# Which engine makes the low halves of the split weights: VectorE alone in four phases

## The chip, the cores and the metric

One core of a Trainium2 chip runs the whole program. The metric is the device time of one execution in microseconds, median of several runs. The engines are named as the profile names them: PE (TensorE, matrix products; PEld is its weight load), DVE (VectorE), ACT (ScalarE), POOL (GpSimd) and SP, whose queue issues the weight DMAs.

## What is computed

Three transformer layers over 256 tokens of width 1024, all float32. Layer 0 mixes with eight forget-gate heads and eight sparse heads, layer 1 with sixteen causal heads, and each is followed by a gated FFN of width 2816 with a short convolution. Layer 2 mixes with eight latent-attention heads and four mLSTM heads, and is followed by a mixture of 32 experts and a gated embedding.

```python
def conv_glu_ffn(x, w_up, conv_w, conv_b, w_down):
    h = x @ w_up
    g, u = h[..., :D_FF], h[..., D_FF:]
    g = conv(g, conv_w) + conv_b            # causal, three taps, per channel
    return (jax.nn.silu(g) * u) @ w_down

for layer in range(2):
    h = rmsnorm(x, attn_norm[layer])
    x = x + mixer(h @ w_in[layer]) @ w_out[layer]
    x = x + conv_glu_ffn(rmsnorm(x, ffn_norm[layer]), w_up[layer], ..., w_down[layer])
x = rmsnorm(x, final_norm)
h = rmsnorm(x, norm_mix_g)
x = x + concat(latent_attention, mlstm)(h @ w_in_2) @ w_o
x = x + moe(rmsnorm(x, norm_ffn_g))
x = x + (p @ w_ple) * sigmoid(rmsnorm(x, norm_ple_g) @ w_ple_gate)
return rmsnorm(x, final_norm_g)
```

## The kernel before

**Split products.** A dense product is made of three: with a = ah + al and w = wh + wl, where the high parts are roundings to the PE's fast float32 type and the low parts are the remainders, it is ah·wh + al·wh + ah·wl. A unit is one 128 x 1024 piece of weight. `Weights.high` (L291) has ACT round a unit into `wh`, and `Weights.low` (L300) subtracts that from the loaded weight `w` into `wl`. Both inputs of that subtraction lie in SBUF. The subtraction is cut in eighths of a unit's first free dimension: `W.eighths` of eight go to POOL and the others to DVE, two instructions one behind the other in program order, each on its own engine. Some buffers of both kinds are a spare tile called `extra`, and the output projections use `xhw`, `xlw` and `wo` for some units.

**Who sets the share.** `W.eighths` begins at 0, is 3 from L1486 on for the first mixer, takes `SHARE[0]` = 3 when a mixer is done (L1578, so for the FFN behind it), `SHARE[1]` = 5 at the last of an FFN's 22 column blocks (L1313), `SHARE[2]` = 4 in the second mixer (L1594), `SHARE[3]` = 4 in the third (L1676), and 3 for the last gate (L2457). In the tail of every output projection (L1198) and in a forced piece at the end of the first FFN (L1303) it is 0.

**Phases.** The first mixer with its output projection (to about 150 us), the first FFN (to 331), the second mixer and its output projection (to about 460), the second FFN (to 649), the third mixer's input projection (to 706), its output projection and router (to about 780), and then the experts and the gate. An FFN (`ffn`, L1235) goes over 22 blocks of 128 columns. `up(j)` multiplies two units, `gate` does convolution and gating on ACT and DVE (the DVE steps write `more`, three times `c`, and `al`), and `down(j)` multiplies one unit by `ah` and `al`. That is 72 matmuls of 128x256 for a block. The four phases that the change touches have 66 + 32 + 66 + 12 units.

**Order of the work.** All instructions are placed by a planner at build time: `Clock` (L64) gives each a cost (L142 to L146: DVE 0.07 us + 1.04 ns for each column of a subtraction, POOL 0.1 us + 2.2 ns) and keeps a time for each engine. `prepare` (L320) converts units ahead of their use, and `tick` (L432) places steps of the attention and norm chains between matmuls, but none while the planned time of ACT or DVE is over `LEAD` (8, 4 and 4 us) ahead of the PE's (L445). So other costs can give another order. Each engine runs its instructions strictly in the order placed. `W.done` frees a weight's slot after its last low part, and the next weight DMA on SP's queue waits for that.

In the profile all records carry the line of the recording helper, L205, so rows are told apart by their tiles.

Of the kernel before, what the change touches and what calls it, by code (L numbers as in the profile page):

```python
# [26 lines left out]
NEG = -1e30  # L27
SW = 2064
EARLY = (2.0, 3.0, 1.5)
SHARE = (3, 5, 4, 4)  # L30
SIDE = (2, 6, 3)
FIRST = 3
WARM = 10
# [315 lines left out]
def kc(t, k, c):  # L349
    return t[:, :k * c].rearrange("p (k c) -> p k c", k=k)  # L350
# [3 lines left out]
def tile_two_blocks(ctx: ExitStack, tc: tile.TileContext, a: dict, out: bass.AP):  # L354
# [6 lines left out]
    def st(shape, dt=F32, tag=None, name=None, bufs=1):  # L361
        return sb.tile(list(shape), dt, tag=tag or name, name=name or tag, bufs=bufs)
# [3 lines left out]
    def bank(i):  # L366
        t = ps.tile([128, 512], F32, tag=f"b{i}", name=f"bank{i}", bufs=1)
        if i == 7:
            last_misc[0] = t
        return t  # L370
# [5 lines left out]
    def mm(o, l, r, start, stop):  # L376
        nc.tensor.matmul(o, l, r, start=start, stop=stop, skip_group_check=True)
# [4 lines left out]
    def tt(o, x, y, op=OP.mult, eng=None):  # L382
        (eng or nc.vector).tensor_tensor(o, x, y, op=op)
# [17 lines left out]
    W = Weights(nc, sb, NS)  # L401
# [7 lines left out]
    lay = [0]  # L409
# [22 lines left out]
    def tick(most=None, lead=None):  # L432

        n = 0
        most = most or MOST[lay[0]]
        lead = lead or LEAD[lay[0]]
        for w in [w for w in waiting if w[1] <= state]:
            waiting.remove(w)
            go(w[0])
        for p in [p for p in parting if p[1] <= state]:  # L440
            parting.remove(p)
            W.drop(*p[0])
        W.prepare(clk)
        for e in list(side):
            if n == most or max(clk.at["act"], clk.at["dve"]) > clk.now() + lead:  # L445
                break
            if e[1] <= clk.now() + SLACK[lay[0]] and step(e):
                n += 1
        return n
# [3 lines left out]
    def pause():  # L453

        if tick(1, 1e9):
            idle[0] = 0
            return
        idle[0] += 1
        if idle[0] > 400:
            raise RuntimeError("side work is stuck")  # L460
        clk.floor = clk.now() + 0.1
# [23 lines left out]
    def free(*names):  # L485
        busy.difference_update(names)
        for n in names:
            freed[n] = clk.last
# [9 lines left out]
    def drain():  # L498
        while side or waiting:
            pause()  # L500
# [478 lines left out]
    def norm_of(sums, rope=None):  # L979

        yield sums.left[-1][1]
        rsqrt(rt, sums.done()[:, :, 0], D, 2)
        yield
        spread(rb, rt)
        if rope is not None:
            rope_scaled(rope, rb)


    def product(o, u, m, start, bh=None, bl=None):

        bh, bl = (xh, xl) if bh is None else (bh, bl)
        h, l = W.take(u, clk)
        hv, lv = kc(h, KD, 128), kc(l, KD, 128)
        until(l)
        for k in range(KD):
            mm(o[:m], hv[:, k, :m], bh[:, k], start and k == 0, False)
            mm(o[:m], hv[:, k, :m], bl[:, k], False, False)
            mm(o[:m], lv[:, k, :m], bh[:, k], False, k == KD - 1)
            if k % 2:
                tick()  # L1000
# [3 lines left out]
    def halves_of(b):  # L1004
        return b.rearrange("p (a t) -> p a t", a=2)
# [3 lines left out]
    def dense_bank(keep=False):  # L1009

        dn[0] ^= 1
        n = ("dense", dn[0])
        while n in busy:
            pause()
        b = halves_of(bank(5 + dn[0]))
        if keep:
            busy.add(n)
            owner[b.tensor.name] = n
        return b
# [125 lines left out]
    def out_proj(us, pair_done, mixed):  # L1145

        nonlocal xh, xl
        for i, t in enumerate(("xh", "xl")):  # L1150
            W.places[us[2 + i]] = sb.tile([128, 2, 1024], F32R, tag=t, name=f"{t}w", bufs=1)
        room = HOLD[lay[0]]
        if room:
            W.places[us[4]] = W.hold("wo", (128, 2, 1024), F32R)
        begun = []
        for m in (0, 2):
            b = dense_bank()
            begun.append((b, us[m:m + 2], list(range(KD))))
        own = None
        for u in us[:2]:  # L1160
            W.pairs[u] = W.take(u, clk)
        W.more = 2 + room
        W.once = ONCE
        while any(left for _, _, left in begun):
            if not own and len(side) <= SIDE[lay[0]] and not waiting and W.parted[1] > us[4 + room]:
                own = next((n for n in BK[2:] if n not in busy and freed.get(n, 0.0) <= clk.now()), None)
                if own:
                    busy.add(own)
                    begun.append((halves_of(bank(own[1])), us[4:5 + room], list(range(KD))))
            k = None  # L1170
            for b, un, left in begun:
                if W.parted[1] <= un[-1]:
                    continue
                ws = [W.pairs[u] for u in un]
                k = next((k for k in left if ("mixed", lay[0], k) in state and
                          (not side or max(clk.ready(ml[:, k]), clk.ready(ws[-1][1])) <= clk.now() + SLACK[lay[0]])), None)
                if k is not None:
                    break
            if k is not None:
                for i, (h, l) in enumerate(ws):  # L1180
                    hv, lv = kc(h, KD, 128), kc(l, KD, 128)
                    mm(b[:, i], hv[:, k], mh[:, k], len(left) == KD and i == 0, False)
                    mm(b[:, i], lv[:, k], mh[:, k], False, False)
                for i, (h, l) in enumerate(ws):
                    mm(b[:, i], kc(h, KD, 128)[:, k], ml[:, k], False, len(left) == 1)
                left.remove(k)
                tick()
            else:
                pause()
        for u in us[:4]:  # L1190
            W.take(u, clk)
        W.more, W.once = 0, False
        drain()
        mixed()
        if lay[0] < 2:
            xh = st([128, KD, T], F32R, tag="xh", name="xh")
            xl = st([128, KD, T], F32R, tag="xl", name="xl")
        e, W.eighths = W.eighths, LASTS  # L1198
        for m in range(0, KD, 2):
            if m < 4:  # L1200
                b = begun[m // 2][0]
            else:
                b = begun[2][0] if own and m == 4 else dense_bank()
                for i in range(2):
                    if own and m == 4 and i <= room:
                        W.take(us[m + i], clk)
                    else:
                        product(b[:, i], us[m + i], 128, i == 0, mh, ml)
            tt(X[:, m:m + 2], b, X[:, m:m + 2], OP.add)
            if not m:  # L1210
                for u in us[5 + room:6 + 2 * room]:
                    W.force(0, u)
                    W.force(1, u)
            if m == NXT and room and lay[0] < 2:
                W.force(0, us[7] + 1)
                W.force(1, us[7] + 1)
            pair_done(m)
            if m == 4 and room:
                W.drop("wo")
            if m == 4 and own:  # L1220
                free(own)
        W.eighths = e
# [12 lines left out]
    def ffn(l, us, norm, pair_done, limit_after):  # L1235
# [21 lines left out]
        def up(j):  # L1257
            b = halves_of(bank(4 + j % 3))
            product(b[:, 0], us[j][0], 128, True)
            product(b[:, 1], us[j][1], 128, False)  # L1260
            if j == 0:
                finish(norm)
            g = gate(j, b)
            next(g)
            go(g)
# [43 lines left out]
        def ups(j):  # L1309
            if j == NJ - 9:  # L1310
                W.limit = limit_after
            if j == NJ - 1:
                W.eighths = SHARE[1]  # L1313
            up(j)
# [259 lines left out]
    def mixed(*names):  # L1574
        def go_on():
            dbg("mh" if not lay[0] else f"mh{lay[0]}", mh.bitcast(F32))
            W.limit = NS
            W.eighths = SHARE[0]  # L1578
            W.drop(*names)
        return go_on  # L1580

    sums = Sums()
    out_proj(PL["wo0"], fed_by(lambda k: col("ffn_norm", k), sums), mixed("V", "aP", "aPT", "aQ", "a1", "a2"))
    W.drop("mh", "ml")
    dbg("X1", X)
# [7 lines left out]
    lay[0] = W.phase = 1  # L1593
    W.eighths = SHARE[2]  # L1594
    norm = norm_of(sums, 0)
# [18 lines left out]
    for i in range(8):  # L1614
# [5 lines left out]
        go(moba(i, qks[i % 3], b))  # L1620
    sums = Sums()
    out_proj(PL["wo1"], fed_by(lambda k: col("ffn_norm", 8 + k), sums), mixed("V", "aP", "aPT", "aQ", "aR"))
    W.drop("mh", "ml")
    dbg("X3", X)
# [50 lines left out]
    W.limit = NS - 9  # L1675
    W.eighths = SHARE[3]  # L1676
    cq = halves_of(aP[:, 1536:2048])
# [916 lines left out]
```

## Time and profile before

| | |
|---|---|
| median of 3 runs | 1067.29 us (1064.92 to 1072.06) |
| the profiled execution | 1074.68 us, of it 1073.0 us span |
| PE, DVE, ACT, POOL busy in the span | 998.9, 632.5, 476.1, 357.4 us |
| mean granted clock of TensorE | 0.962 |

The span runs from the first instruction to the last. A busy PE is not a PE at its peak: matmuls are pipelined, a 128x256 one is recorded with about 280 ns and the next begins some 115 ns behind it. So the number of matmuls in a stretch tells more than the busy time. The granted clock is a share of full speed, 0.5 being 1.2 GHz and 1.0 being 2.4 GHz.

### The profile page before, as it was taken

How to read it: one execution, taken by the hardware profiler on the slowest of the kernel's cores; microseconds unless marked ns; L12 is line 12 of the kernel's file. 1: busy time of each engine (PE TensorE's matmuls, PEld its weight loads, DVE VectorE, ACT ScalarE, POOL GpSimd, SP SyncE). 2: the span in 40 equal slices, each digit the busy share in tenths (PEclk: the TensorE clock that was granted, in tenths of full speed). 3: DMA queues.
4: the chain of work that ended last, by engine and by line, in shares of the span. 5: the costliest groups of instructions: out<-in, count | busy, mean ns of one | idle time of the engine just before them, and what ended most of it. 6: DMA issues, size and time to landing. Idle time of an engine off the chain costs nothing. (4 is left out here: it accounts for less than half of the span.)

```text
span 1073.0 us, 19846 instructions
## 1 busy us (share of the span) xinstructions
PE 998.9 (93%) x7612; PEld 857.0 (80%) x7612; DVE 632.5 (59%) x1285; ACT 476.1 (44%) x866; POOL 357.4 (33%) x365
## 2 busy tenths in 40 slices
PE   7999999999998998999999999879989999798686
PEld 7888899999998987999999999867874554353456
DVE  4798577676677589676666687567552221021056
ACT  5555565455554555464554555644512121121053
POOL 7424154445545433344544453341310000000032
PEclk8999999999999999999999999979989999998888
DMA  7653299465511541497556103330879999999951
GB/s 214 167 193 119 79 345 345 155 218 171 183 41 38 160 144 54 162 370 254 182 172 210 53 1 93 105 118 23 311 277 334 351 412 410 410 412 411 401 183 40
DMA packets 135318, 223.14 MB, mean 208 GB/s; under 512 B 11161, under 2 KB 103473, under 8 KB 135217
## 3 DMA queue, kind: packets, MB, share of 16 engines
q1 hardware_dynamic: 134673, 221.80, 58.4%
q8 instruction: 62, 1.02, 0.4%
q14 instruction: 39, 0.32, 0.1%
q10 hardware_dynamic: 544, 0.00, 0.0%
HBM read 220.73 MB, written 1.05 MB: 207 GB/s over the span
## 5 line engine op out<-in xcount | busy, mean ns | idle before, releaser
L205 PE MATMUL bank<-xh,wh 128*128 128x256 f32 x808 | 233.9, 289 | 3.0 <-ACT wh L205 3.0
L205 PE MATMUL bank<-xl,wh 128*128 128x256 f32 x808 | 228.3, 283 | 0.8 <-DVE xl L205 0.8
L205 PE MATMUL bank<-xh,wl 128*128 128x256 f32 (+1 forms) x752 | 212.6, 283 | 5.1 <-DVE wl L205 5.1
L205 POOL TENSOR_TENSOR wl<-w,wh 128x384 fp32r<-128x384 f32 (+2 forms) x97 | 141.1, 1461 | 199.9 <-ACT wh L205 92.7
L205 ACT ACTIVATE wh<-w 128x1024 fp32r<-128x1024 f32 x153 | 159.5, 1050 | 8.6 <-PE bank L205 5.4
L205 PEld LDWEIGHTS bank<-xh,wh 128*128 128x128 f32 x808 | 155.4, 192 | 5.5 <-ACT wh L205 3.3
L205 PEld LDWEIGHTS bank<-xl,wh 128*128 128x128 f32 x808 | 155.1, 192 | 2.5 <-DVE xl L205 1.4
L205 PEld LDWEIGHTS bank<-xh,wl 128*128 128x128 f32 (+1 forms) x752 | 143.7, 191 | 6.0 <-DVE wl L205 6.0
L205 PE MATMUL bank<-xh,extra 128*128 128x256 f32 (+1 forms) x552 | 141.7, 283 | 0.0
L205 PE MATMUL bank<-w,xg 128*32 128x512 f32 (+1 forms) x512 | 93.9, 647 | 17.8 <-DMA w<-in_w_up_e_dram 11.6
L205 PEld LDWEIGHTS bank<-xh,extra 128*128 128x128 f32 (+1 forms) x552 | 98.9, 188 | 0.7 <-issue 0.7
L205 POOL TENSOR_TENSOR gate<-w,gate 128x384 fp32r<-128x384 f32 x8 | 11.5, 1466 | 253.2 <-DMA w<-in_w_down_e_dram 235.7
L205 DVE TENSOR_TENSOR wl<-w,wh 128x640 fp32r<-128x640 f32 (+3 forms) x102 | 87.7, 861 | 9.9 <-ACT wh L205 6.9
L205 PEld LDWEIGHTS bank<-w,xg 128*32 128x32 f32 (+1 forms) x512 | 30.4, 127 | 72.0 <-issue 71.6
L205 ACT ACTIVATE c<-more,v,cw 128x256 f32<-128x256 f32 x44 | 26.5, 603 | 132.9 <-DVE more L205 132.9
L205 POOL TENSOR_TENSOR extra<-w,wh 128x384 fp32r<-128x384 f32 (+2 forms) x49 | 64.5, 1317 | 41.8 <-ACT wh L205 32.4
L205 DVE TENSOR_TENSOR more<-bank,more 128x512 f32<-128x512 f32 x44 | 30.3, 689 | 77.2 <-PE bank L205 77.2
L205 DVE SCALAR_TENSOR_TENSOR sg<-sg,ws,bank 128x256 f32<-128x256 f32 x11 | 5.3, 480 | 115.9 <-ACT sg L205 115.9
L205 PE MATMUL bank<-al,wh 128*128 128x256 f32 x256 | 71.7, 280 | 1.2 <-DVE al L205 1.2
L205 PE MATMUL bank<-ah,wh 128*128 128x256 f32 x256 | 71.4, 279 | 0.0
L205 PE MATMUL bank<-xl,extra 128*128 128x256 f32 (+2 forms) x248 | 69.8, 281 | 0.0
L205 PE MATMUL bank<-ah,extra 128*128 128x256 f32 x256 | 65.7, 280 | 1.5 <-DVE extra L205 1.5
(484 smaller groups left out, 2385.4 us busy)
## 6 DMA issues: line engine op xcount, KB each, us to landing
w<-in_w_up_dram SPq DMA_DIRECT2D x44, 1024.0 KB
w<-in_w_gate_e_dram SPq DMA_DIRECT2D x64, 512.0 KB
w<-in_w_up_e_dram SPq DMA_DIRECT2D x64, 512.0 KB
w<-in_w_down_e_dram SPq DMA_DIRECT2D x32, 1024.0 KB
w<-in_w_down_dram SPq DMA_DIRECT2D x22, 1024.0 KB
w<-in_w_in_odd_dram SPq DMA_DIRECT2D x12, 1024.0 KB
w<-in_w_in_even_dram SPq DMA_DIRECT2D x9, 1024.0 KB
w<-in_w_in_dram SPq DMA_DIRECT2D x5, 1024.0 KB
```

What stands on the lines that cost most here:

```text
L205: return f(*a, **kw)
```

## The change

In both FFNs, the second mixer and the third mixer's input projection DVE makes the whole low part of each unit in one 128x1024 subtraction, and POOL none of it. In the first mixer, the third mixer's output projection and the last gate the shares stay as they were.

```diff
-SHARE = (3, 5, 4, 4)
+SHARE = (0, 0, 0, 0)
...
         own = None
+        if lay[0] == 2:
+            W.eighths = 4
         for u in us[:2]:
             W.pairs[u] = W.take(u, clk)
```

The second piece stands in `out_proj`: `lay[0]` is the layer, so it gives the third mixer's output projection the 4 that it had from `SHARE[3]` before.

## Rows read from the trace of the kernel before

**Rows 1.** The page's first part: busy us of each engine (share) xinstructions.

```profile
PE 998.9 (93%) x7612; PEld 857.0 (80%) x7612; DVE 632.5 (59%) x1285; ACT 476.1 (44%) x866; POOL 357.4 (33%) x365
```

**Rows 2.** Windows by stage: us, busy us (xcount) of five engines, clock, DMA share, GB/s.

```profile
160.00:320.00 160.00, 160.00 (x1377) 160.00 (x1376) 112.23 (x156) 81.88 (x116) 78.21 (x57) 1.00 0.56 189
320.00:345.00 25.00, 20.71 (x157) 19.89 (x156) 21.07 (x33) 14.12 (x25) 12.75 (x9) 0.93 0.00 1
345.00:460.00 115.00, 110.88 (x931) 103.51 (x930) 83.16 (x169) 60.73 (x137) 47.75 (x32) 0.99 0.43 143
460.00:640.00 180.00, 179.56 (x1526) 179.56 (x1527) 127.25 (x185) 92.82 (x131) 86.17 (x64) 0.99 0.54 177
640.00:706.00 66.00, 59.71 (x447) 55.35 (x446) 47.44 (x106) 38.73 (x60) 24.75 (x21) 0.97 0.31 97
```

**Rows 3.** PE's waits from 135 to 706 us: us in total, times, longest.

```profile
PE bank L205 <- DVE wl L205: 6.0, 3, 3.2
PE bank L205 <- DVE extra L205: 4.9, 3, 1.7
PE bank L205 <- DVE al L205: 1.2, 2, 0.6
PE bank L205 <- DVE xl L205: 1.1, 3, 0.5
PE bank L205 <- DVE rt L205: 1.0, 2, 0.6
```

**Rows 4.** Timeline of PE: start, us, instruction, idle time before it and releaser.

```profile
326.93 0.39 PE L205 MATMUL bank<-ah,wl 128*128 128x256 f32 x1 [1.71 <-DVE wl L205]
...
644.65 0.39 PE L205 MATMUL bank<-ah,extra 128*128 128x256 f32 x1 [1.46 <-DVE extra L205]
...
679.59 0.38 PE L205 MATMUL bank<-xh,wl 128*128 128x256 f32 x1 [3.22 <-DVE wl L205]
```

**Rows 5.** DVE's groups by shape, 160 to 320 us: busy us, mean ns | idle before.

```profile
L205 DVE TENSOR_TENSOR c<-c,more 128x256 f32<-128x256 f32 x20 | 25.4, 1271 | 0.0
L205 DVE TENSOR_TENSOR wl<-w,wh 128x640 fp32r<-128x640 f32 x28 | 23.0, 821 | 0.1
L205 DVE SCALAR_TENSOR_TENSOR c<-more,cw,c 128x256 f32<-128x256 f32 x39 | 18.9, 485 | 1.2 <-ACT c L205 0.5
L205 DVE TENSOR_TENSOR al<-c,ah 128x256 fp32r<-128x256 f32 x20 | 14.7, 733 | 9.7 <-ACT ah L205 9.7
L205 DVE TENSOR_TENSOR more<-bank,more 128x512 f32<-128x512 f32 x20 | 13.8, 690 | 36.7 <-PE bank L205 36.7
```

**Rows 6.** A DVE group by shape over the whole span, away from the FFNs.

```profile
L205 DVE TENSOR_TENSOR more<-more,more 128x256 f32<-128x256 f32 x6 | 2.3, 422 | 5.8 <-ACT more L205 5.8
```

**Rows 7.** POOL's largest group by shape, 160 to 320 us.

```profile
L205 POOL TENSOR_TENSOR wl<-w,wh 128x384 fp32r<-128x384 f32 x28 | 40.3, 1441 | 59.5 <-DVE c L205 36.0 <-ACT wh L205 22.6 <-DVE extra L205 0.8
```

**Rows 8.** Timeline of DVE: a low part that DVE makes whole.

```profile
136.86 1.22 DVE L205 TENSOR_TENSOR wl<-w,wh 128x1024 fp32r<-128x1024 f32 x1
```

**Rows 9.** Timeline of DVE at the first FFN's end.

```profile
320.78 0.56 DVE L205 TENSOR_TENSOR extra<-w,wh 128x384 fp32r<-128x384 f32 x1
321.38 1.68 DVE L205 TENSOR_TENSOR c<-c,more 128x256 f32<-128x256 f32 x1
323.60 1.17 DVE L205 TENSOR_TENSOR al<-c,ah 128x256 fp32r<-128x256 f32 x1 [0.55 <-ACT ah L205]
324.69 2.17 DVE L205 TENSOR_TENSOR wl<-w,wh 128x384 fp32r<-128x384 f32 x1
```

**Rows 10.** Timeline of DVE, the second mixer's output projection.

```profile
429.50 1.78 DVE L205 TENSOR_TENSOR xlw<-w,xlw 128x512 fp32r<-128x512 f32 x1
```

**Rows 11.** Timeline of POOL in the same stretch.

```profile
428.99 1.74 POOL L205 TENSOR_TENSOR wo<-w,wo 128x512 fp32r<-128x512 f32 x1
```

**Rows 12.** Timeline of DVE in the third mixer, ahead of the longest wait.

```profile
675.26 2.60 DVE L205 SCALAR_TENSOR_TENSOR bX<-bX,v 128x253 f32<-128x253 f32 x3 [0.33 <-ACT bX L205]
```

**Rows 13.** Windows, columns as above: two stretches with a lowered clock.

```profile
339.00:343.00 4.00, 4.00 (x22) 4.00 (x23) 1.53 (x9) 0.40 (x2) 0.00 (x0) 0.57 0.00 0
...
711.00:729.00 18.00, 16.64 (x57) 12.88 (x58) 5.25 (x11) 6.78 (x18) 5.40 (x5) 0.53 0.23 76
```

## The prediction

> **What bounds the kernel now.** I read the page's first part, then windows by stage, then PE's waits, then the timelines around the waits. On the page PE is busy for 93% of the span, DVE for 59%, POOL for a third [rows 1]. The windows tell where that is no slack and where it is [rows 2]. In the 160 us of the first FFN's steady part PE has no idle time: 1377 matmuls, so 0.116 us each, and the second FFN's stretch is the same but for 0.4 us at its start. A block of 72 matmuls takes 72 x 0.116 = 8.4 us, and no faster low part can shorten that. The change must earn its time elsewhere: 4.3 us of PE idle time at the first FFN's end, 4.1 in the second mixer, 6.3 in the third's input projection [rows 2]. The waits name what ends these: from 135 to 706 us PE waits 6.0 + 4.9 us for low parts (`wl` and `extra`, three waits each) and 1.2 us for `al`, and 2.1 us for `xl` and `rt`, small DVE results [rows 3]. That is 14.2 us, nearly all of it DVE's, though DVE is not full.
>
> **Why DVE is late without being full.** In the FFN DVE's step `c<-c,more` takes 1.27 us for 256 columns, its `al` step 0.73 [rows 5]; the same kind of subtraction or product of two SBUF tiles, 256 columns, takes 0.42 where POOL is idle [rows 6]. In the output projection the two engines go in lockstep: DVE's half of a low part takes 1.78 us and POOL's half of the neighbouring unit 1.74 [rows 10, 11], where DVE alone makes a whole unit in 1.22 [rows 8]. So a DVE instruction with two SBUF inputs and a POOL subtraction stand in each other's way, one after the other, and the halves of a low part are not made side by side.
>
> A page of the Trainium skill speaks against the change. GPSIMD Engine Reference, § 3.1 gives 4497 ns for a two-input addition of 2048 float32 columns on GpSimd and 2293 on VectorE, each for itself; scaled to 384 and 640 columns (my estimate from that page) a shared low part would be done after some 0.85 us, against 1.22 for DVE alone, and the sum below would turn into a loss. Another page decides it the other way: SBUF — State Buffer, § Who interferes with whom says that VectorE with two SBUF inputs and a GpSimd instruction that reads SBUF exclude each other for a whole instruction. The rows of the last paragraph agree with the second page (1.78 against 1.74 us in lockstep).
>
> **The change, part by part.**
> *DVE's load.* A block of the FFN costs DVE now 3 x 0.82 (low parts) + 0.69 (`more`) + 2 x 0.485 + 1.27 (`c`) + 0.73 (`al`) = 6.1 us [rows 5], and afterwards 3 x 1.22 + 0.69 + 0.97 + 0.42 + 0.42 = 6.2 us [rows 5, 6, 8]. That is 6.2 of 8.4 us: three longer instructions and two that are no longer held up cancel. If the freed time did not come, it would be 7.2 us, still under the PE. So the two steady stretches, 160 and 180 us, change by nothing; PE hides it.
> *POOL.* It loses some 1.44 us for each unit [rows 7]. Nothing waited for POOL alone there, so this is worth nothing by itself. The slot of a weight comes free with the low part, so DMAs start no later.
> *First FFN's end*, where POOL has five eighths. From the row `extra<-w,wh` to the end of `wl<-w,wh` the DVE chain gains 1.68 - 0.42 (`c`), 1.17 - 0.42 (`al`) and 2.17 - 1.22 (`wl`), and pays 1.22 - 0.56 (`extra`): 1.26 + 0.75 + 0.95 - 0.66 = 2.3 us [rows 6, 8, 9]. The stalls there are 1.71 [rows 4] and about half of the 1.2 for `al` [rows 3], 2.3 us. I take 2.0, since what is next, the second low part, is close behind; between 0 and 2.3.
> *Second FFN's end*, the same pattern: 1.46 [rows 4] and the other half of `al`'s 1.2; I take 1.8 of 2.1.
> *The third mixer's wait of 3.22 us* [rows 4]. Three DVE steps ahead of the awaited low part take 2.60 us [rows 12]; a scalar-times-tile step is 0.485 [rows 5], so about 1.1 us of that is a block by POOL. The low part itself then goes from about 1.75 (as in rows 10) to 1.22. I take 1.1 + 0.5 = 1.6; the rest waits for ACT and stays.
> *The third `wl` wait*, 6.0 - 1.71 - 3.22 = 1.1 us in the second mixer [rows 3, 4]: I take 0.9, as it has the same form.
> *The other two waits for `extra`*, 4.9 - 1.46 = 3.4 us [rows 3, 4]. One is just behind the first FFN, where the low part is already made whole and POOL's additions for the norm stay; the other is in the output projection, where a unit of the lockstep loses 1.78 - 1.22 = 0.55 us [rows 8, 10]. I take 0.8 in all.
> *`xl` and `rt`*, 2.1 us [rows 3]: chains of small DVE steps that POOL's low parts interrupt; I take 0.9.
> *The clock.* Behind such stalls TensorE is granted half its speed, 1.2 instead of 2.4 GHz, for a while: from 339 us on, 4 us at a mean of 0.57 with 22 matmuls, where 4 / 0.116 = 34 would fit; 4 x 0.43 = 1.7 us are lost [rows 13]. There are four such stretches in the four phases (339, 428, 462 and 681 us), 6.8 us. If the stalls before them halve I expect half of it back, 3.4; between 0 and 6.8.
> *The new line* in `out_proj` keeps the third output projection at its old share: no cost, as a number is set at build time.
>
> Sum: 2.0 + 1.8 + 1.6 + 0.9 + 0.8 + 0.9 + 3.4 = 11.4 us. The profiled execution took 1074.68 us (span 1073.0), 7.4 over the median of the runs shown. The terms are stalls of fixed size, so I take them off either: 1063.3 for an execution like the profiled one, and 1067.3 - 11.4 = 1056 us for the median.
>
> **The rivals.**
> *The stalls are passed on (about 1063 us).* DVE works in order, and what PE needs next may be late behind the longer low part, or ACT's rounding is what is really late: at the first FFN's end DVE itself waits 0.55 us for ACT [rows 9]. Then perhaps a third of the sum remains, 4 us. For it: half of the waits lie in mixers where PE and the attention chains wait for each other. Against it: the two FFN ends are pure DVE chains.
> *The planner places the work worse (about 1080 us); this is the one on the other side.* For the planner a low part in the second mixer costs DVE 0.07 + 1024 x 1.04 ns = 1.14 us instead of 0.60, and the 24 units of its input projection and some of its output projection, say 28, add 15 us to DVE's planned time in a stage of 115 us. As no side step is placed while DVE's planned time is over 4 us ahead, the attention chains may be placed later, and the output projection waits for the last. It decides once DVE's planned load passes the PE's; at worst the whole 15 us come on the path, less the 3.8 us won at the FFN ends, plus one more lowered clock stretch of 1.7: +13. Against it: DVE is busy for 83 of these 115 us [rows 2], 15 more do not fill it; and the planner believed that POOL makes its half in 0.1 + 512 x 2.2 ns = 1.23 us, so by its account the low part comes no later than before.
> *The halves did run side by side (about 1075 us).* Then each of the eight waits for `wl`, `extra` and `al` [rows 3] grows by 0.4 us (1.22 against 0.82 [rows 5, 8]) for each of about two low parts ahead of it, 6.4 us, and a clock stretch more. The lockstep rows [rows 10, 11] speak plainly against it. It is what the Trainium skill's GPSIMD Engine Reference, § 3.1, would lead to.
> *More comes back (about 1047 us).* Behind 711 us, in the unchanged output projection, the clock is low for 18 us at a mean of 0.53 [rows 13], 8.5 us lost. If the faster input projection leads into it without that, this is added to the sum. The shares there stay, so I give it little.
>
> **How the numbers follow.** My forecast has a chance of 0.52, with its own range from 1050 to 1062; the passed-on stalls 0.26, the planner 0.10, side by side 0.04, more 0.08. The likeliest gives 1056. All waits of rows 3 and all four clock stretches would be 14.2 + 6.8 = 21 us, 1046: the low end. The high end, 1071, takes in the passed-on stalls down to nothing and a small planner's loss. What a measurement of this kernel can tell from no change is about 1%, 10.7 us: faster by more than that is under 1056.6. Some 0.6 of the forecast and all of the last rival lie there: 0.31 + 0.08 = 0.39. Slower by over 1% is the planner's rival and a little of the third: 0.10. The rest, 0.51, is within 1%.
>
> **What would show it.** Right: `c<-c,more` and `al` at 0.42 us in the FFNs, low parts at 1.22, POOL busy for some 120 us instead of 357, 0.116 us a matmul as before, PE's waits for `wl`, `extra` and `al` from 135 to 706 us at 5 us instead of 12, and one or two fewer low-clock stretches. Wrong: new waits of PE for `aP`, `mh` or `ml` in the second mixer (planner), waits of the same length under other names (passed on), or `c` still over 1 us.

## The result and the profile after

The changed kernel takes 1054.7 us (median, 1051.2 to 1060.1) against 1066.7 for the kernel before in the same comparison: a ratio of 0.9882, 95% interval 0.9848 to 0.9915, so 12.0 us less. In a second comparison it was 1058.8 us, a ratio of 0.9892 (0.984 to 0.9945). The forecast was 1056.

The first part of the page of the changed kernel, as in [rows 1]:

```profile
span 1049.4 us, 19312 instructions
PE 982.1 (94%) x7612; PEld 842.5 (80%) x7612; DVE 622.6 (59%) x1285; ACT 479.2 (46%) x868; POOL 109.7 (10%) x191
```

POOL lost 248 us of work, and DVE, which took all of it over, is busy for 10 us *less*. So what DVE gained in the instructions that were held up outweighs the longer low parts. The groups of DVE by shape in the first FFN show it (160 to 316 us, changed kernel; busy us, mean ns, idle before), beside [rows 5] with 1271 and 733 ns:

```profile
L205 DVE TENSOR_TENSOR wl<-w,wh 128x1024 fp32r<-128x1024 f32 x28 | 34.1, 1217 | 0.0
...
L205 DVE TENSOR_TENSOR al<-c,ah 128x256 fp32r<-128x256 f32 x19 | 8.1, 426 | 9.2 <-ACT ah L205 9.2
L205 DVE TENSOR_TENSOR c<-c,more 128x256 f32<-128x256 f32 x19 | 8.0, 419 | 0.0
```

The windows by stage of the changed kernel (columns as in [rows 2]; the stages come earlier, so the bounds are shifted):

```profile
160.00:316.00 156.00, 156.00 (x1342) 156.00 (x1342) 107.67 (x151) 80.79 (x113) 0.00 (x0) 1.00 0.57 193
316.00:341.00 25.00, 23.22 (x198) 23.02 (x197) 21.86 (x36) 15.58 (x26) 3.44 (x3) 1.00 0.02 3
341.00:450.00 109.00, 107.29 (x924) 100.79 (x922) 81.05 (x172) 60.06 (x136) 3.51 (x3) 1.00 0.48 157
450.00:625.00 175.00, 174.90 (x1500) 174.73 (x1501) 122.31 (x179) 91.71 (x129) 0.12 (x1) 1.00 0.53 178
625.00:691.00 66.00, 62.85 (x488) 58.80 (x486) 50.80 (x112) 43.97 (x71) 9.14 (x9) 1.00 0.31 97
```

In the first row PE has no idle time and runs a matmul in 156.00 / 1342 = 0.116 us, as before. What was won lies in the other rows: 1.8 us of PE idle time at the first FFN's end, 1.7 in the second mixer, 3.2 in the third's input projection, where [rows 2] give 4.3, 4.1 and 6.3, and a clock of 1.00 throughout. Of the 3.2 us, 3.0 are the beginning of a wait that comes further below (688.0 to 694.1 us). PE's waits from 135 to 691 us, beside [rows 3]:

```profile
PE bank L205 <- DVE extra L205: 2.8, 2, 1.8
PE bank L205 <- ACT mh L205: 0.5, 1, 0.5
PE bank L205 <- DVE xl L205: 0.3, 1, 0.3
PE bank L205 <- ACT aPT L205: 0.3, 1, 0.3
PE bank L205 <- ACT aP L205: 0.2, 1, 0.2
```

No wait for `wl` or `al` of this size is left. At the first FFN's end DVE's chain of [rows 9] (`extra`, `c`, `al`, `wl`) now reads as follows (timeline of DVE, changed kernel):

```profile
318.89 1.22 DVE L205 TENSOR_TENSOR extra<-w,wh 128x1024 fp32r<-128x1024 f32 x1
320.03 0.42 DVE L205 TENSOR_TENSOR c<-c,more 128x256 f32<-128x256 f32 x1
320.99 0.43 DVE L205 TENSOR_TENSOR al<-c,ah 128x256 fp32r<-128x256 f32 x1 [0.54 <-ACT ah L205]
321.33 1.22 DVE L205 TENSOR_TENSOR wl<-w,wh 128x1024 fp32r<-128x1024 f32 x1
```

From start to end that is 322.55 - 318.89 = 3.7 us, where [rows 9] give 326.86 - 320.78 = 6.1.

**One caution for reading the two profiles side by side.** The spans differ by 23.6 us, the medians by 12.0. The profiled execution of the kernel before (1074.68) lies 8.0 us above its median, that of the changed kernel (1051.18) 3.5 us under its own. So differences between the two traces overstate the gain about twofold, and what a part is worth must come from timed runs. With that said, the traces place the difference so (differences of the times at which PE begins or ends a stage): first mixer 0.9 us, first FFN 2.8, second mixer with output projection 6.4, from there to the second FFN's first down product 2.3, second FFN 2.6, third mixer and router 6.8, all the rest 1.8. A second trace of the same changed kernel (run e11, 1058.97 us) gives, in the same order, 2.5, 2.8, 4.9, 2.3, 2.6, 1.0 and -0.3. So the FFNs' shares are firm, and the third mixer's 6.8 us is one execution's.

One wait has a new name. Timeline of PE in the third mixer (start, us, instruction, idle time and releaser), first the kernel before, then the changed kernel, and DVE ahead of it there:

```profile
712.37 3.75 PE L205 MATMUL bank<-w,bX 128*128 128x128 f32 x16 [5.46 <-issue]
```

```profile
694.14 1.51 PE L205 MATMUL bank<-ident,aP 128*128 128x128 f32 x6 [6.13 <-DVE aP L205]
```

```profile
689.57 1.15 DVE L205 TENSOR_TENSOR wl<-w,extra 128x512 fp32r<-128x512 f32 x1
690.64 1.75 DVE L205 TENSOR_TENSOR xhw<-w,xhw 128x512 fp32r<-128x512 f32 x1
692.31 0.68 DVE L205 TENSOR_TENSOR xlw<-w,xlw 128x512 fp32r<-128x512 f32 x1
692.91 0.68 DVE L205 TENSOR_TENSOR extra<-w,wh 128x512 fp32r<-128x512 f32 x1
693.51 0.17 DVE L205 RECIPROCAL ri<-sm 128x4 f32<-128x4 f32 x1
693.71 1.01 DVE L205 TENSOR_SCALAR aP<-aP,ri 128x128 f32<-128x128 f32 x4
```

In the new order the step that scales the attention weights (`aP`) stands behind four low parts of the output projection, two of them still held up by POOL's halves (1.15 and 1.75 us, where the next two take 0.68). PE waits 6.1 us. That is not 6.1 us more than before: the kernel before has 5.5 us of idle time in the same stage, from 706.9 us on and so just outside the stretch of [rows 3], while DVE makes low parts of the same output projection. The profile names no releaser there (`issue`).

### The profile page after: what moved, and what is told of

Read it like the earlier page. It is cut to its first block, busy times and chain, and to the rows that moved or that the text cites. A ratio compares the mean times of both kernels' runs of the same rounds, so it can differ in the third digit from the quotient of the medians.

```text
span 1049.4 us, 19312 instructions
## 1 busy us (share of the span) xinstructions
PE 982.1 (94%) x7612; PEld 842.5 (80%) x7612; DVE 622.6 (59%) x1285; ACT 479.2 (46%) x868; POOL 109.7 (10%) x191
## 5 line engine op out<-in xcount | busy, mean ns | idle before, releaser
L205 DVE TENSOR_TENSOR wl<-w,wh 128x1024 fp32r<-128x1024 f32 (+2 forms) x102 | 120.0, 1178 | 8.1 <-ACT wh L205 6.5
L205 DVE TENSOR_TENSOR extra<-w,wh 128x1024 fp32r<-128x1024 f32 (+2 forms) x51 | 60.7, 1191 | 3.3 <-ACT wh L205 3.3
L205 ACT ACTIVATE extra<-w 128x1024 fp32r<-128x1024 f32 (+4 forms) x54 | 53.5, 995 | 1.0 <-PE bank L205 0.9
L205 PE MATMUL bank<-ah,wl 128*128 128x256 f32 x192 | 53.9, 281 | 0.0
```

Source lines behind the costliest of these rows:

```text
L205: return f(*a, **kw)
```

## The experiments

Two things change at once: which engine makes the low parts, and, since the planner is told of other costs, the order of the instructions. In the programs as built about 3% of PE's instructions stand elsewhere than before, and 4 to 5% of DVE's and ACT's. My theory: the gain is DVE's, freed of POOL's subtractions. Rivals: the gain is the new order's; or a POOL instruction as such holds DVE up, whatever it does.

**The new instructions in the old order, and the reverse.** In the first, the planner is told of shared halves, so the order is that of the kernel before, and the instruction issued is a whole one on DVE (`W.whole` is set from the end of the first mixer up to the third output projection, where the change applies). In the second the planner is told of a whole one, and the shared halves are issued.

```diff
 # e3_old_order (in Weights.low)
+            if self.whole and cut < n:
+                self.nc.clock.issue("dve", "tensor_tensor", [z[:, :cut]], [x[:, :cut], y[:, :cut]])
+                self.nc.clock.issue("pool", "tensor_tensor", [z[:, cut:]], [x[:, cut:], y[:, cut:]])
+                self.nc.vector.real.tensor_tensor(z, x, y, op=OP.subtract)
...
 # e4_new_order (in Weights.low)
+            if self.whole and cut < n:
+                self.nc.clock.issue("dve", "tensor_tensor", [z], [x, y])
+                self.nc.vector.real.tensor_tensor(z[:, :cut], x[:, :cut], y[:, :cut], op=OP.subtract)
+                self.nc.gpsimd.real.tensor_tensor(z[:, cut:], x[:, cut:], y[:, cut:], op=OP.subtract)
...
```

> The planner is charged for the shared low parts as before, so that the order on every engine is that of before, but the instructions issued are the whole DVE subtractions. Port: most of the gain is there without the new order, ratio 0.988 to 0.992. Order: ratio 0.998 to 1.002.

> The reverse: the planner is charged for whole DVE subtractions, so that the order is that of the changed kernel, but the instructions issued are the shared ones of before (3, 5, 4 eighths on POOL). Port: no gain, ratio 0.998 to 1.006, and the step c of the FFN still takes 1.25 us. Order: the gain is there, ratio 0.988 to 0.992.

Old order, DVE alone: 1050.4 us, a ratio of 0.9848 (0.9795 to 0.99). New order, shared: 1068.6 us, 1.0014 (0.999 to 1.0039). The whole gain is there without the new order (e3 came out better than the 0.988 to 0.992 expected), and the new order alone gives nothing. In the second, DVE's two groups have the lengths of [rows 5] again (DVE by shape, 162 to 320 us, e4):

```profile
L205 DVE TENSOR_TENSOR c<-c,more 128x256 f32<-128x256 f32 x19 | 24.1, 1271 | 0.0
L205 DVE TENSOR_TENSOR al<-c,ah 128x256 fp32r<-128x256 f32 x19 | 14.0, 735 | 9.2 <-ACT ah L205 9.2
```

So the engine decides, and not the order. The old order has no wait for `aP` in the third mixer, but in its place the idle time of the kernel before (5.5 us, releaser `issue`). From the second FFN's end to the gather behind the router e3 takes 140.2 us, the changed kernel 142.5 in its first trace and 148.3 in its second, the kernel before 149.3. Whether e3 is faster than the changed kernel on the whole its interval doesn't tell.

**What of POOL's instruction holds DVE up?** As e3, but DVE makes its share and POOL writes zeros over the other columns, at the same places in the program; that share of the low parts is left out.

```diff
 # e5_pool_writes, against e3
-                self.nc.vector.real.tensor_tensor(z, x, y, op=OP.subtract)
...
+                    self.nc.vector.real.tensor_tensor(z[:, :cut], x[:, :cut], y[:, :cut], op=OP.subtract)
+                self.nc.gpsimd.real.memset(z[:, cut:].bitcast(F32), 0.0)
...
```

> The order of before; POOL's share of each low part in the four phases is a memset to zero instead of a subtraction, so that POOL writes the same columns and reads nothing (the low parts lack that share: this part of the computation is left out); DVE makes its share as before. If POOL's reads of SBUF are what stands in DVE's way: c<-c,more and al in the FFNs at 0.42 us and DVE's 640 columns at 0.82, time at or below that of e3 (1050). If any POOL instruction does: c stays over 0.9 us.

1044.0 us in a single run; as DVE makes only its share here, the time isn't comparable with e3's, and what counts is the length of DVE's steps. In the first FFN (by shape, 160 to 316 us, e5) POOL writes 36 times for 0.42 us into `wl` alone, and DVE is not held up:

```profile
L205 DVE TENSOR_TENSOR al<-c,ah 128x256 fp32r<-128x256 f32 x19 | 8.1, 425 | 11.2 <-ACT ah L205 11.2
L205 DVE TENSOR_TENSOR c<-c,more 128x256 f32<-128x256 f32 x19 | 8.0, 419 | 0.0
```

```profile
L316 POOL MEMSET wl<- 128x384 f32 x36 | 15.1, 420 | 84.8 <-PE bank L205 84.8
```

Is that because the writes are short and miss DVE's steps? One block tells: of e5 (timelines of DVE and POOL),

```profile
207.78 0.42 DVE L205 TENSOR_TENSOR c<-c,more 128x256 f32<-128x256 f32 x1
```

```profile
207.58 0.42 POOL L316 MEMSET extra<- 128x384 f32 x1 [2.43 <-PE bank L205]
```

and the same block of the kernel before:

```profile
207.76 0.82 DVE L205 TENSOR_TENSOR wl<-w,wh 128x640 fp32r<-128x640 f32 x1
208.50 1.24 DVE L205 TENSOR_TENSOR c<-c,more 128x256 f32<-128x256 f32 x1
```

```profile
207.80 1.65 POOL L205 TENSOR_TENSOR wl<-w,wh 128x384 fp32r<-128x384 f32 x1 [3.54 <-ACT wh L205]
```

Half of the `c` step of e5 lies under a POOL write, and it takes 0.42 us all the same. It is no exception: each of the 19 `c` steps from 160 to 316 us lies in part under a POOL write, and they take 416 to 426 ns. Before, POOL's subtraction is issued just behind DVE's `wl`, lasts past its end, and `c` then takes 1.24. So it is not POOL at work that stops DVE but POOL at work on inputs (two here; one input was not tried). This is what the Trainium skill's page SBUF — State Buffer, § Who interferes with whom, says of VectorE with two inputs in SBUF: it contends with a GpSimd instruction that reads SBUF and not with one that only writes; the rows agree.

**Which phases?** Only the FFNs, only the two mixers, and only the last blocks of the FFNs:

```diff
 # e1_ffn_only (with the piece in out_proj)
-SHARE = (3, 5, 4, 4)
+SHARE = (0, 0, 4, 4)
 # e2_mixers_only (with the piece in out_proj)
+SHARE = (3, 5, 0, 0)
 # e7_ffn_end
+SHARE = (3, 0, 4, 4)
```

> SHARE (0, 0, 4, 4): DVE alone makes the low parts in the two FFNs only. Theory 'port' (a DVE instruction with two SBUF inputs and a POOL subtraction exclude each other, and the gain is the waits that this made): the two FFN ends give 3.8 us by the prediction's sum, and one or two of the lowered clock stretches 1.7 us each, so some 5 us, ratio 0.995; the steady stretches keep 0.116 us a matmul. Rival 'order' (the gain is the planner's new order, which differs most in the mixers): nothing, ratio 1.000.

> SHARE (3, 5, 0, 0) with the new line: DVE alone in the second mixer and the third's input projection only. Port: the rest of the sum, 6 to 7 us, ratio 0.994. Order: nearly all of the 12 us, ratio 0.989.

> SHARE (3, 0, 4, 4): only the second number goes to 0, for the last column block of each FFN and nothing else. The prediction's terms for the two FFN ends: 2.0 + 1.8 = 3.8 us and perhaps one lowered clock stretch of 1.7, ratio 0.995 to 0.997. If the ends' waits are passed on: ratio 0.998 to 1.000.

The ratios are 0.9933 (0.9903 to 0.9963), 0.9961 (0.9933 to 0.999) and 0.9964 (0.9939 to 0.9989): 7.1, 4.2 and 3.8 us by the ratios, 5.9, 4.0 and 5.1 by the medians. The FFNs came out better than expected (0.995), the mixers worse (0.994). FFNs and mixers add up to 11.3 us by the ratios and 9.9 by the medians, so to most of the 12.0. The traces are far sharper on the FFNs. From the first FFN's first down product to its last PE takes 170.45 us before and in e2 170.44, and in e1, e3, e7 and both traces of the changed kernel 167.64; in the second FFN 170.55 in the first two and 167.92 in all the others. So an FFN gains 2.8 and 2.6 us, all of it at its end, as e7 shows: the steady part gives nothing. PE's waits from 135 to 700 us in e7 show that its edit reaches just what it was meant to reach; the 3.2 us of the third mixer are still there:

```profile
PE bank L205 <- DVE wl L205: 4.3, 2, 3.2
PE bank L205 <- DVE extra L205: 3.4, 2, 1.7
```

**No low part on POOL at all.** If POOL's reads only do harm, the change stops too early. Here DVE makes all of them, once by the shares (so the planner makes a new order), and once with the order of the kernel before, as in e3:

```diff
 # e6_all_dve, against the changed kernel: the first mixer, the third's output projection, the last gate
-            W.eighths = 4
+            W.eighths = 0
...
-    W.eighths = 3
+    W.eighths = 0
 # e8_old_order_all, against e3: whole in every phase
-        self.whole = False
+        self.whole = True
```

> The changed kernel with DVE alone in the first mixer, the third output projection and the last gate as well: no low part on POOL anywhere. Port: sharing is no help there either; the last gate's low parts (1.08 + 1.47 us, one behind the other) go to 1.22, worth 1 to 2 us at the end of the path, so 0 to 4 us under the changed kernel, ratio 0.984 to 0.988. Rival 'DVE is full in the mixers' (busy 19 of 20 us from 60 to 80 us): the first mixer loses 2 to 5 us, ratio 0.990 to 0.993.

> As e3 (order of before, whole DVE subtractions), in all phases of the kernel. Port: 0 to 4 us under e3, ratio 0.981 to 0.985. DVE is full in the mixers: 2 to 5 us over e3, ratio 0.987 to 0.990.

By the shares: 1067.8 us, a ratio of 1.0005 (0.9978 to 1.0031). All that the change won is gone, which no theory of mine expected. In the old order: 1042.2 us (1041.4 to 1043.7), 0.9784 (0.9736 to 0.9832), the fastest of all, and better than the 0.981 to 0.985 expected. So DVE isn't too full for the work. The two do the same work; only the order is another. Windows of the first 150 us, first e6, then e8:

```profile
0.00:150.00 150.00, 131.07 (x998) 118.66 (x999) 102.66 (x276) 78.53 (x175) 28.69 (x99) 0.97 0.50 153
```

```profile
0.00:150.00 150.00, 140.74 (x1113) 129.38 (x1114) 109.39 (x295) 86.32 (x186) 31.08 (x100) 0.99 0.58 183
```

In the same time e6 gets through 115 matmuls fewer; at 0.116 us each that is 13.3 us, about half of the 25.6 between the medians. The traces agree: e6 is 13.3 us behind e8 at the first FFN's first down product, still 13.4 at the second FFN's end, and 23.1 at the gather behind the router. The first mixer and the third lose it, and nothing between. The largest waits of PE in e6's first 150 us (us in total, times, longest), then those of e8 (to 140 us):

```profile
PE bank L205 <- ACT a L205: 4.5, 3, 3.8
PE bank L205 <- DVE v L205: 3.2, 1, 3.2
PE bank L205 <- DVE extra L205: 3.2, 1, 3.2
```

```profile
PE bank L205 <- ACT wh L205: 3.0, 1, 3.0
PE bank L205 <- POOL ident L205: 1.4, 1, 1.4
PE bank L205 <- DVE aQ L205: 1.3, 1, 1.3
PE bank L205 <- DVE v L205: 1.2, 1, 1.2
```

Waits of this size for `a` and `extra` are not among those of e8: in e6 steps of the first mixer stand elsewhere. `LEAD`, by which my planner rival explained such a loss, is not the cause there: built with its limit lifted in the first mixer, e6 is the same program, instruction for instruction.

**Which of the planned costs makes the bad order?** The same work as e8 three times more: with DVE's planned time charged for the whole unit, but the low part planned ready as if shared (e9); the other way round (e10); and in exactly the order of the changed kernel (e12).

```diff
 # e9_load_charged, against e8
+                self.nc.clock.at['dve'] += (n - cut) * x.shape[2] * 1.04e-3 ...
 # e10_ready_charged, against e8
-                self.nc.clock.issue("dve", "tensor_tensor", [z[:, :cut]], [x[:, :cut], y[:, :cut]])
-                self.nc.clock.issue("pool", "tensor_tensor", [z[:, cut:]], [x[:, cut:], y[:, cut:]])
+                self.nc.clock.issue("dve", "tensor_tensor", [z], [x, y])
+                self.nc.clock.at['dve'] -= (n - cut) * x.shape[2] * 1.04e-3 ...
 # e12_changed_order_all: the changed kernel, and e8's issue in Weights.low
```

> No low part on POOL anywhere, as e6 (1067.8) and e8 (1042.2), in a third order: the planner charges DVE's time for the whole subtraction, but takes the low part as ready when the shared one would be. If the order of before is one that the kernel's hand-set priorities were chosen for, so that any other loses: 1053 to 1070. If only e6's order is an unlucky one: 1040 to 1050.

> The same work in a fourth order: the planner takes the low part as ready when the whole subtraction would be, but charges DVE's time for the shared one. Expected as for e9: 1053 to 1070 if any order but that of before loses, 1040 to 1050 if e6's is an unlucky one.

> No low part on POOL anywhere, in the order of the changed kernel, which in the first mixer is that of before. If e6's loss against e8 is made in the first mixer's order: 1044 to 1050. If the order of the later phases makes it: 1055 to 1066.

e9: 1065.0 us, 0.9964 (0.9939 to 0.999). e10: 1056.8, 0.9883 (0.9852 to 0.9914). e12: 1048.8, 0.9833 (0.9796 to 0.987). So one and the same set of instructions (but for one to three table loads of ACT) takes 1042, 1049, 1057, 1065 or 1068 us by its order alone, and each of the two truer costs makes it worse. DVE's planned time costs most, some 23 us; the other alone costs some 15, so the two don't add up to e6's 26. e9 too loses most of it in the first 150 us (993 matmuls). e12, whose first mixer is planned as before, is only 0.7 us behind e8 at the second FFN's end and 7.0 at the gather. Part of the loss is TensorE's clock: the mean granted clock of the runs falls in the same order, 0.975, 0.974, 0.971, 0.966 and 0.964. Time times the missing share, an estimate of what the low clock costs, is 26, 27, 31, 36 and 39 us, so about half of the 25. Which steps in the order make the waits I could not settle.

**The changed kernel once more**, beside these, so that they can be compared:

```diff
 # e11_changed_again: the change as it is
-SHARE = (3, 5, 4, 4)
+SHARE = (0, 0, 0, 0)
```

> The changed kernel once more beside the others: ratio 0.985 to 0.991.

1058.8 us, 0.9892 (1049.4 to 1060.3). e12 has the same order and a median 10 us lower, and e8 has one 8 us under e3's, which is the same step in the old order. Both pairs point to a cost of the low parts that POOL keeps in the changed kernel, but in both the two intervals overlap; the four runs of e8 all lie below the four of e3.

## Why the prediction was right, and where not

**The mechanism** held step by step: `c` and `al` at 0.42 us, low parts at 1.22, POOL at 110 us of busy time (120 forecast), and 0.116 us a matmul in the steady FFN. e3 and e4 show that the freed DVE carries the gain, and e5 narrows it to POOL's reads, which [rows 10, 11] had left open.

**DVE's load** was to stay level (6.1 to 6.2 us a block). It is 107.67 of 156 us, 69%, against 112.23 of 160, 70%: level, and hidden by PE. (The load that I gave for the case that the freed time did not come, 7.2 us, adds up to 7.3; nothing hangs on it.)

**The two FFN ends**, 2.0 + 1.8 = 3.8 us, were right in kind and too small. DVE's chain at the first gets 2.4 us shorter, 2.3 forecast. e7 measures 3.8 us by its ratio, but with an interval from 1.2 to 6.5, and 5.1 by the medians; the traces give 2.8 + 2.6 = 5.4 us. The reason stands in PE's timeline before, at the second end:

```profile
641.89 0.28 PE L205 MATMUL bank<-ah,wh 128*128 128x256 f32 x1
642.81 0.39 PE L205 MATMUL bank<-al,wh 128*128 128x256 f32 x1 [0.64 <-DVE al L205]
644.65 0.39 PE L205 MATMUL bank<-ah,extra 128*128 128x256 f32 x1 [1.46 <-DVE extra L205]
644.87 0.28 PE L205 MATMUL bank<-ah,wh 128*128 128x256 f32 x1
```

From 641.89 to 644.87 us are three steps, which take 3 x 0.116 = 0.35 us in the steady part, so 2.6 us are lost. I had added up the idle times, 0.64 + 1.46 = 2.1. Most of the difference is that they count from the recorded end of a matmul (0.28 us long, or 0.39), and not from where the next one would have begun.

**The mixers' terms**, 1.6 + 0.9 + 0.8 + 0.9 = 4.2 without the clock, measure 4.2 (e2; 1.1 to 7.1, and 4.0 by the medians). But the inner accounts differ. Of the third mixer's 3.2 us I left half to ACT; the wait is gone altogether, but the stage as a whole is hardly shorter. From the second FFN's end to the gather its time times its granted clock, an estimate of what it would take at full clock, is 149.3 x 0.91 = 136 us before, 142.5 x 0.96 = 137 and 148.3 x 0.91 = 135 in the two traces of the changed kernel, and 140.2 x 0.94 = 132 in e3. (e8, in the old order too, gives 137.5 x 0.96 = 132.) So in the new order the term of 1.6 us did not arrive, and in the old one some 4 us did. PE's waits for `wl`, `extra` and `al` fell from 12.1 to 2.8 us, more than to the 5 forecast. One wait for `extra`, behind the first FFN, stays at 1.8 us, as I said it would.

**The clock**: I took half of 6.8 us back. In its four places more came back; on the whole nothing did that the runs show. In the first trace of the changed kernel all four stretches of half clock between 339 and 681 us are gone, in the second (e11) three of them, and a stretch of 3.4 us stands at 333 us. But a stretch of 6.8 us follows the wait for `aP` in both, and behind it the two differ. The windows around these places, changed kernel, first trace:

```profile
690.00:698.00 8.00, 3.85 (x14) 2.62 (x16) 7.86 (x18) 4.99 (x9) 3.10 (x3) 0.57 0.74 263
711.00:729.00 18.00, 17.24 (x127) 14.29 (x124) 10.18 (x36) 8.51 (x29) 1.28 (x1) 1.00 0.34 132
```

and of the second trace:

```profile
711.00:729.00 18.00, 18.00 (x114) 14.65 (x113) 10.37 (x36) 8.62 (x29) 1.28 (x1) 0.87 0.19 64
```

From 690 to 830 us the kernel before has 27.3 us of half clock, the first trace 10.2 and the second 30.7. Over whole executions the granted clock is 0.969 in the mean of 57 runs of the kernel before and 0.968 in that of eight runs of the changed kernel. Time times the missing share (my estimate) is 33.0 and 34.2 us, with an uncertainty of some 5 us in the difference; so the 3.4 us is not shown, nor quite excluded. The runs of one kernel differ by their clock: the eight of the changed kernel go from 1049.4 us at 0.979 to 1060.3 at 0.961.

**The sum** of 11.4 us against the measured 12.0 is so close in part by luck: the FFN ends were put 1.6 us too low, the third mixer's 1.6 did not arrive, and the clock's 3.4 is not seen on the whole.

**The rivals.** Passed-on stalls: not on the whole (12.0 us and not 4), but in the third mixer of the changed kernel they were, as its 136, 137 and 135 us tell. Halves side by side: out, by e4's 1271 and 735 ns; the Trainium skill's GPSIMD Engine Reference, § 3.1, has rates of each engine for itself, and in this kernel's rows they don't add up. More comes back: the 711 us stretch did in the changed kernel's first trace (mean clock 1.00) and in the second only in part (0.87, with more low stretches behind it). The planner: I gave it 0.10 and it did not decide here, yet it was the largest lever in sight. I put its danger into the second mixer and into `LEAD`. The changed kernel escaped the larger part of it because it leaves the first mixer's shares alone; e6, which changes them too, does 85 matmuls fewer than the changed kernel's 1083 in the first 150 us, 9.9 us of the 13 that it is slower. I had worked out the planner's effect as a cost in time on DVE, when it is a choice among orders that are 25 us apart.

## What to carry to other kernels

Where two engines share an elementwise job, look at the *neighbours* of that job: a step that is three times as long as its like elsewhere (1.27 against 0.42 us) says that the helper is taking the time from the engine that it helps. When a build-time planner decides the order, time the new instructions in the old order as well (e3 and e8 need a few lines for it), or the price of an order is put down to the instructions. And before you compare two traces, see where each profiled execution lies among its kernel's runs, and trace one kernel twice: two traces of the changed kernel put 6.8 and 1.0 us on the same stage.

## What I had not expected of the hardware

A POOL instruction that only writes SBUF (0.42 us for 128x384) does not delay a DVE step with two SBUF inputs under which it runs (`c` 419 ns in the mean of 19 steps, as without POOL), where one that reads two tiles makes it three times as long (1271 ns).
